# A two-layer decoder on one core: modulation chunks moved from the FFN up-projections to the attention, first tiles as unsplit fp32 products, x transposed at the end

## The chip, the core and the metric

The kernel runs on one core of one Trainium2 chip. The core has five engines that run side by side, each through its own list of instructions in order: TensorE (PE in the profile; its weight loads are PEld), VectorE (DVE), ScalarE (ACT), GpSimd (POOL) and SyncE (SP). SP issues nearly all loads. Instructions of different engines wait for one another by semaphores. The metric is the device time in microseconds (us), the median of several executions; smaller is better.

## The reference, cut to what matters

A batch of one sequence of 256 tokens with 1024 channels goes through two layers. Layer 0 mixes tokens by dilated causal attention (16 heads, three window sizes), layer 1 by gated linear attention (GLA, four heads, chunks of 64 tokens). Behind each mixer stands a gated feed-forward network (FFN) with a causal convolution over three tokens. Every one of the four sub-layers is modulated by a conditioning vector c:

```
mod = silu(c) @ w_ada[i] + b_ada[i]
sh1, sc1, g1, sh2, sc2, g2 = split(mod, 6)
h = rmsnorm(x, norm_mix[i]) * (1.0 + sc1) + sh1
y = attention(h) if i == 0 else gla(h)
x = x + g1 * y
h = rmsnorm(x, norm_ffn[i]) * (1.0 + sc2) + sh2
u = conv(h @ w_up[i]); a, b = split(u, 2)
x = x + g2 * ((silu(a) * b) @ w_down[i])
...
return rmsnorm(x, norm_final)
```

All is float32. The up-projection is 1024 to 5632, the down-projection 2816 to 1024, w_ada is 1024 to 6144 in each layer.

## The kernel before, in words

Activations lie transposed: channels on the 128 partitions, the 256 tokens along the free dimension, so x and h are eight tiles of 128x256. TensorE multiplies float32 values that are split in a high part (fp32r, a shorter float32) and a low part, the rest. `split` loads 1 MB of weights into a buffer `raw` (L159), ScalarE casts it to `whi` (L165) and VectorE subtracts to get `wlo` (L168), each in two halves of 128x1024. `mm3` (L174 to L176) then issues three matmuls: hi by hi, hi by lo, lo by hi. An unsplit fp32 matmul exists too; the kernel uses it for small things such as the sums of squares.

`raw` comes from a pool of four buffers, `whi` and `wlo` from pools of three. The matmul results go to eight banks of PSUM in three groups of tags: p (2 banks), s (3) and t (3). Where no tag is named, tags go round in a fixed cycle.

The modulation vector is made in 48 chunks, `ada_chunk` (L129 to L150), 24 a layer. A chunk loads 1 MB of w_ada into one of the same four `raw` buffers (L133). VectorE multiplies and sums each of its two halves against silu(c) (L138), and ScalarE adds the bias and writes `mod`, a column of 128 values (L146, L148). `next_ada` issues the next chunk in turn. Where the calls stand in the program decides which stage pays for them on the loads, on VectorE and on the buffers.

A norm works thus. After every tile of the residual stream is updated (`residual`, L273), `add_square` (L195) squares it on ScalarE and adds up squares. `rstd_of` (L183) sums over channels by three unsplit matmuls with a matrix of ones (`ms`, L186), then ScalarE does Ln (L188) and Exp (L190). For each of the eight tiles `normed` (L246) forms `xr` on VectorE (L250), `hhi` on ScalarE (L252) and `hlo` on VectorE (L253). While TensorE waits for the first of these, `keep_warm` (L259) issues six small matmuls without use.

The stages, in order. Layer 0's attention goes over eight pairs of heads, u = 0 to 7; in each it projects q, k (`pqk`) and v (`pv`), copies them out of PSUM (`evacuate`, L424; `by_group`, L442), and `attend` forms scores, exponentials, the normalised probabilities `pn` (L400, L401), their transposes on TensorE (L405), copies of these, `pt` (L406), and the output `po`. `project` (L515) is the output projection (`py`) with the residual. `ffn` (L539) runs 22 tiles of the up-projection: 48 matmuls into one bank `pab`, then the convolution, silu and gate product; then the down-projection (`pd`, four pairs of output tiles, four loads each). The GLA follows with the projections of v (`pv`, L649), the gates (`log_gates`), the states of four heads, four gate tiles (`gate`, L741, result `pr`), and its own `project`; then layer 1's `ffn`. At the end each tile of x is scaled by rstd (L786 to L790) and written, still transposed, by four DMAs (L791).

The order of instructions on each engine is fixed when the program is built, by a scheduler that places work by its own estimates within the dependencies; `behind(...)` is a constraint on it, which issues what stands inside after the named instructions. `chain[kt]` are the last instructions that made tile kt of h.

Of the kernel before, what the change touches and what calls it, by code (L numbers as in the profile page):

```python
# [18 lines left out]
P = 128  # L19
D = 1024  # L20
# [37 lines left out]
def trunk(ctx: ExitStack, tc: tile.TileContext, I, out):  # L58
# [136 lines left out]
    def add_square(kt):  # L195

        sq = tmp.tile([P, T], F32, tag="sq", name="sq")
        i = nc.scalar.activation(sq, x[kt], AF.Square)
        part = 0 if kt < 3 else 1 if kt < 7 else 2
        if kt in (0, 3, 7):  # L200
            sums[part] = sq
        else:
            acc = tmp.tile([P, T], F32, tag="sqacc", name="sqacc")
            (nc.gpsimd if kt < 3 else nc.vector).tensor_tensor(acc, sums[part], sq, op=ALU.add)
            sums[part] = acc
        if kt < 6:
            squared[0] = i
# [56 lines left out]

    def all_normed(l, sub):
        r = rstd_of([sums[0], sums[1], sums[2]])
        with behind(norm_ops[0]):
            keep_warm(6)
        return [normed(l, sub, r, kt) for kt in range(KT)]

    def residual(l, sub, kt, ps):
        g = mod[l, 3 * sub + 2, kt]
        i = nc.vector.scalar_tensor_tensor(x[kt], ps, g[:, 0:1], x[kt], op0=ALU.mult, op1=ALU.add)  # L273
        if kt < 6:
            squared[1] = i
# [80 lines left out]
    def attend(u, q, k, v, bias):  # L356
# [32 lines left out]
        for h in range(2):  # L389
# [6 lines left out]
            for r in (2 * h, 2 * h + 1):  # L396

                f = m[:, 12 + r : 13 + r]
                pn = att.tile([P, KEYS], F32, tag="pn", name="pn", bufs=3)
                nc.vector.tensor_scalar(grouped(pn[:, 0:T]), by_residue(prob[r][:, 0:T]), f, None, op0=ALU.mult)  # L400
                nc.vector.tensor_scalar(pn[:, T:KEYS], prob[r][:, T + r : KEYS + r], f, None, op0=ALU.mult)  # L401
                t = bank("t", "t")
                for j in range(3):
                    c = slice(P * j, P * j + P)
                    nc.tensor.transpose(t[:, c], pn[:, c], ident)  # L405
                (nc.vector.tensor_copy if r % 2 else nc.scalar.copy)(pt[:, r, :], t[:, 0:KEYS])  # L406
        po = bank("po", "t")
# [16 lines left out]
    def evacuate(q, k, g, pq, pk):  # L424
# [3 lines left out]
        if g:  # L428
            nc.scalar.mul(q[g], pq, 0.125)
            return nc.vector.tensor_copy(k[g], pk)  # L430
        qh, ql = q[0]
# [23 lines left out]
    for u in range(NPAIR):  # L455
# [53 lines left out]
        attend(u, q, k, v, bias)  # L509
        if u == 1:  # L510
            for n in range(2):
                next_ada()
    o = list(zip(o_hi, o_lo))

    def project(src, o, l, sub):  # L515

        ends = []
        for n in range(4):
            w = split(src[n], 2048)
# [10 lines left out]
            ends.append(e)  # L530
            for i in range(2):
                residual(l, sub, 2 * n + i, ps[i][:, T * i : T * i + T])
                add_square(2 * n + i)

    project(I["w_out_a"], o, 0, 0)
    at_pool.__exit__(None, None, None)


    def ffn(l):  # L539
        h = all_normed(l, 1)  # L540
        with tc.tile_pool(name=f"ffn{l}", bufs=2) as pool:
            g_hi = [pool.tile([P, T], F32R, tag=f"ghi{i}", name="ghi", bufs=1) for i in range(NFF)]
            g_lo = [pool.tile([P, T], F32R, tag=f"glo{i}", name="glo", bufs=1) for i in range(NFF)]
            for i in range(NFF):
                with behind(*(squared[:1], chain[3], chain[7])[min(i, 2)]):
                    w = split(I["w_up"][l, i], 2048)
                pab = bank("pab")
                pu = [pab[:, :T], pab[:, T:]]
                for kt in range(KT):
                    for s in range(2):  # L550
# [22 lines left out]
            exp_ln_after(silu)  # L573
            for f2 in range(0, KT, 2):
                pd = [bank("pd") for _ in range(2)]
                for half, f in ((0, 0), (0, 1), (1, 0), (1, 1)):
                    w = split(I["w_down"][l, f2 + f, half], 11 * P)
                    for j in range(11):
                        i = 11 * half + j
                        mm3(pd[f][:, :T], parts(w, P * j), (g_hi[i], g_lo[i]), i == 0, i == NFF - 1)  # L580
                for f in range(2):
                    residual(l, 1, f2 + f, pd[f][:, :T])
                    add_square(f2 + f)
                    if l == 1 and f2 + f < KT - 1:
# [4 lines left out]
    ffn(0)  # L589


# [10 lines left out]
    nc.gpsimd.memset(keep.rearrange("p (n c) -> p n c", c=CH)[:, :, 0:1], 0.0)  # L602
    h = all_normed(1, 0)

# [45 lines left out]
    for n in range(4):  # L650
        with behind(*(squared, chain[5], chain[7], glr_copy)[n]):
            w = split(I["w_v_b"][n], 2048)
            if n > 1:
                next_ada()
        for i in range(2):
            kt = 2 * n + i
# [81 lines left out]

    r_g = []

    def gate(n):  # L741
        w = split(I["w_r_b"][n], 2048)
        pr = bank("pr", "p")
        for kt in range(KT):
            for s in range(2):
                mm3(pr[:, T * s : T * s + T], parts(w, 2 * P * kt + P * s), h[kt],
                    kt == 0 and s == 0, kt == KT - 1 and s == 1)
        if n % 2 == 0:
            r_g.append(gt([P, 4, T], "r4", tag=("C", "cs")[n // 2]))
        nc.scalar.copy(r_g[-1][:, 2 * (n % 2) : 2 * (n % 2) + 2, :], pr.rearrange("p (a b) -> p a b", a=2))  # L750

# [6 lines left out]
    output(2, *s2)  # L758
    gate(0)
    next_ada()  # L760
    output(3, *s3)
    for n in range(1, 4):
        gate(n)
        if n < 2:
            next_ada()
    o = []
    for n in range(4):
        r = r_g[n // 2][:, 2 * (n % 2) : 2 * (n % 2) + 2, :]
        with behind(*norm_ops):
# [9 lines left out]
    exp_ln_after(last_hi)  # L779
    project(I["w_out_b"], o, 1, 0)  # L780
    gl_pool.__exit__(None, None, None)

    ffn(1)

    r = rstd_of([sums[0], sums[1], sums[2]])
    for kt in range(2):  # L786
        nc.gpsimd.tensor_tensor(x[kt], x[kt], r, op=ALU.mult)
    for kt in range(2, KT - 1):
        nc.vector.tensor_tensor(x[kt], x[kt], r, op=ALU.mult)
    nc.vector.scalar_tensor_tensor(x[7], x[7], col(C_NFIN + 7), r, op0=ALU.mult, op1=ALU.mult)  # L790
    for eng, a, b in ((nc.sync, 2, 4), (nc.scalar, 0, 2), (nc.sync, 4, 6), (nc.sync, 6, 8)):  # L791
        eng.dma_start(out[a:b].rearrange("k p t -> p k t"), x_all[:, a:b, :])

# [77 lines left out]
def build(arrays):  # L871
    import concourse.bacc as bacc

    nc = bacc.Bacc("TRN2", target_bir_lowering=False, num_devices=1)
# [4 lines left out]
    out = nc.dram_tensor("out_y", (KT, P, T), F32, kind="ExternalOutput").ap()  # L879
    with tile.TileContext(nc, schedule_with_timeline_sim=True) as tc:  # L880
# [12 lines left out]
```

## Time and profile before

| What | Value |
|---|---|
| median of three runs | 809.89 us (803.45 to 811.63) |
| profiled execution | 807.78 us |
| its span | 806.1 us |
| mean granted TensorE clock | 0.99 |
| PE busy | 782.4 us, 97% of the span |
| DVE busy | 645.4 us, 80% |
| ACT busy | 466.5 us, 58% |
| moved by DMA | 184.70 MB, 229 GB/s in the mean |

The stages lie in the profiled span about so: start and attention 0 to 270 us, output projection to 298, layer 0's up-projection 302 to 423 and down-projection to 487, GLA 491 to 582, its output projection to 609, layer 1's up-projection 613 to 734 and down-projection to 796, the tail to 806.

A row of the list of groups gives line, engine, operation, the tiles written and read, their shapes and the count, then the busy time in us, the mean of one in ns, and the idle time of the engine just before them with what ended it. A row of a timeline gives the start, the length, engine, line, operation and count of one burst. Matmuls are pipelined: the length of one (0.28 us for 256 columns) is longer than the distance between two starts.

### The profile page before, as it was taken

What the parts mean: (1) busy time and instruction counts of PE and PEld (TensorE: products, weight loads), DVE (VectorE), ACT (ScalarE), POOL (GpSimd) and SP (SyncE); (2) the same over time, 40 slices, a digit from 0 to 9 for tenths busy, and PEclk for the clock granted to TensorE, in tenths of its full rate; (3) what the DMA queues carried; (4) which work ended last, traced back from release to release, by engine and by line L of the source; (5) the groups of instructions that cost most, each with busy time, mean ns of one, the idle gap of its engine ahead of it and who ended that gap; (6) DMA issues with size and microseconds to landing.
All of it is one profiled execution on the core that took longest, in us unless ns stands there. A gap on an engine that the chain in (4) does not pass through costs nothing.

```text
span 806.1 us, 15899 instructions
## 1 busy us (share of the span) xinstructions
PE 782.4 (97%) x6464; PEld 752.5 (93%) x6464; DVE 645.4 (80%) x1153; ACT 466.5 (58%) x867; POOL 16.8 (2%) x42
## 2 busy tenths in 40 slices
PE   8999999999999989999999999999999999999995
PEld 6899999999999889999999998889998999999995
DVE  6998977879778769999997877776468999987552
ACT  5566555455545547777766445644556866766551
POOL 1000000000000010000000000000010000000100
PEclk9999999999999999999999999999999999999998
DMA  8998668486596736877647884873343776644521
GB/s 343 416 328 320 225 256 309 164 305 237 205 321 224 262 105 215 313 257 261 222 136 244 285 322 151 327 261 105 105 159 107 281 274 237 252 145 146 188 99 52
DMA packets 32694, 184.70 MB, mean 229 GB/s; under 512 B 5804, under 2 KB 8364, under 8 KB 15982
## 3 DMA queue, kind: packets, MB, share of 16 engines
q1 hardware_dynamic: 32350, 183.44, 63.1%
q8 instruction: 50, 0.82, 0.4%
q10 hardware_dynamic: 272, 0.26, 0.1%
q14 instruction: 22, 0.18, 0.1%
HBM read 182.59 MB, written 1.10 MB: 228 GB/s over the span
## 4 chain that ended last, share of the span: by engine, by line
PE 67%; DVE 14%; DMA 11%; ACT 4%; issue 2%; DVEq 0%; SPq 0%; ACTq 0%
PE pab L176 10%; PE pab L174 10%; PE pab L175 10%; DVE wlo L168 6%; DMA raw<-in_wqk 5%; PE pd L176 4%; PE pd L175 4%; PE pd L174 4%; PE pqk L176 3%; PE pqk L175 3%; PE pqk L174 3%; DMA raw<-in_wv 2%; DVE ada_raw L138 2%; PE py L175 2%; PE py L174 2%
## 5 line engine op out<-in xcount | busy, mean ns | idle before, releaser
L168 DVE TENSOR_TENSOR wlo<-raw,whi 128x1024 fp32r<-128x1024 f32 (+2 forms) x274 | 295.3, 1106 | 56.9 <-ACT whi L165 56.0
L165 ACT CAST whi<-raw 128x1024 fp32r<-128x1024 f32 (+2 forms) x274 | 247.9, 953 | 153.9 <-PE pab L175 50.5
L174 PE MATMUL pab<-hhi,whi 128*128 128x256 f32 x704 | 194.1, 277 | 1.5 <-ACT hhi L252 1.5
L175 PE MATMUL pab<-hlo,whi 128*128 128x256 f32 x704 | 193.9, 276 | 0.5 <-DVE hlo L253 0.5
L176 PE MATMUL pab<-hhi,wlo 128*128 128x256 f32 x704 | 194.0, 276 | 0.4 <-DVE wlo L168 0.4
L174 PEld LDWEIGHTS pab<-hhi,whi 128*128 128x128 f32 x704 | 132.0, 188 | 2.2 <-ACT hhi L252 1.9
L175 PEld LDWEIGHTS pab<-hlo,whi 128*128 128x128 f32 x704 | 132.0, 188 | 0.9 <-DVE hlo L253 0.9
L176 PEld LDWEIGHTS pab<-hhi,wlo 128*128 128x128 f32 x704 | 132.0, 188 | 0.8 <-DVE wlo L168 0.8
L174 PE MATMUL pqk<-hhi,whi 128*128 128x256 f32 x448 | 123.5, 287 | 3.0 <-ACT hhi L252 2.3
L175 PE MATMUL pqk<-hlo,whi 128*128 128x256 f32 x448 | 125.6, 284 | 0.5 <-DVE hlo L253 0.5
L176 PE MATMUL pqk<-hhi,wlo 128*128 128x256 f32 x448 | 125.0, 283 | 0.0
L138 DVE CUSTOM_DVE_ANT_0 ada_raw<-ada_raw,c_bc 128x1024 f32<-128x1024 f32 x96 | 114.1, 1224 | 5.1 <-DMA ada_raw<-in_w_ada 5.0
L176 PE MATMUL pd<-ghi,wlo 128*128 128x256 f32 x352 | 98.0, 280 | 1.5 <-DVE wlo L168 1.5
L175 PE MATMUL pd<-glo,whi 128*128 128x256 f32 x352 | 98.1, 280 | 0.0
L174 PE MATMUL pd<-ghi,whi 128*128 128x256 f32 x352 | 97.7, 279 | 0.0
L174 PEld LDWEIGHTS pqk<-hhi,whi 128*128 128x128 f32 x448 | 83.7, 191 | 4.7 <-ACT hhi L252 2.7
L175 PEld LDWEIGHTS pqk<-hlo,whi 128*128 128x128 f32 x448 | 85.4, 191 | 1.0 <-DVE hlo L253 0.7
L176 PEld LDWEIGHTS pqk<-hhi,wlo 128*128 128x128 f32 x448 | 85.1, 191 | 0.2
L176 PEld LDWEIGHTS pd<-ghi,wlo 128*128 128x128 f32 x352 | 65.8, 187 | 1.7 <-DVE wlo L168 1.7
L175 PEld LDWEIGHTS pd<-glo,whi 128*128 128x128 f32 x352 | 66.0, 188 | 0.0
L174 PEld LDWEIGHTS pd<-ghi,whi 128*128 128x128 f32 x352 | 65.9, 188 | 0.0
L558 ACT ACTIVATE r<-pab,small 128x256 f32<-128x256 f32 x88 | 48.5, 559 | 11.7 <-DVE r L561 11.3
(176 smaller groups left out, 1247.0 us busy)
## 6 DMA issues: line engine op xcount, KB each, us to landing
ada_raw<-in_w_ada SPq DMA_DIRECT2D x47, 1024.0 KB, 6.5
raw<-in_w_up SPq DMA_DIRECT2D x44, 1024.0 KB, 5.1
raw<-in_w_down SPq DMA_DIRECT2D x32, 704.0 KB, 4.2
raw<-in_wqk SPq DMA_DIRECT2D x18, 1024.0 KB, 7.0
raw<-in_wv SPq DMA_DIRECT2D x14, 768.0 KB, 4.6
raw<-in_w SPq DMA_DIRECT2D x7, 960.0 KB, 6.6
raw<-in_w_out_a SPq DMA_DIRECT2D x4, 1024.0 KB, 6.4
raw<-in_w_v_b SPq DMA_DIRECT2D x4, 1024.0 KB, 5.7
```

The lines of the kernel that those rows point to most:

```text
L138: nc.vector.tensor_tensor_reduce(w, w, c_bc, op0=ALU.mult, op1=ALU.add, scale=1.0, scalar=0.0, accum_out=dot,)
L165: copied[0] = nc.scalar.copy(hi[:, c], raw[:, c])
L168: last_lo[0] = nc.vector.tensor_tensor(lo[:, c], raw[:, c], hi[:, c].bitcast(F32), op=ALU.subtract)
L174: mm(ps, a[0], b[0], start=start, stop=False)
L175: mm(ps, a[0], b[1], start=False, stop=False)
L176: return mm(ps, a[1], b[0], start=False, stop=stop)
L558: nc.scalar.activation(r, u[:, :T], AF.Identity, scale=cw[2], bias=col(C_CB + 44 * l + f))
```

## The change

- **Modulation chunks.** Before, attention issues 20 of the 48 (two behind u = 1, three in each later pair), layer 0's up-projection 6, its down-projection 6, the GLA stage 4, layer 1's up-projection 4. The rest are made at the start. After, attention has 28 (four behind u = 1, and a fourth in each later pair), both up-projections none, layer 0's down-projection 6, the GLA stage 2, layer 1's down-projection 4.
- **Three copies to ScalarE.** In `attend` the second part of `pn` (L401, 128x128) and the odd transposes' copies (L406, 128x384), and in `evacuate` the copy of k (L430), move from VectorE.
- **Unsplit first tiles.** At three norms (both FFNs and the GLA) the first weight tile behind the norm is multiplied before rstd is known. `scale` writes x times the modulation's scale to `early_x` on ScalarE as each tile of x is done, `shift_columns` puts the shift in as column 257, `load_early` loads the weights, and `products` issues 16 unsplit fp32 matmuls of 257 columns into two banks `early`. Four of them stand ahead of the sums `ms`, twelve behind. `whole` then multiplies the result by rstd on VectorE and adds the shift's column on ScalarE. In the FFNs this is tile 0 of the up-projection, with tag p; in the GLA it is gate tile 0, with tag t. `keep_warm` isn't called any more. The `split` of tile 1 is issued behind `chain[0]`, that of tile 2 behind `chain[5]`, later ones behind `chain[7]`; `whole` in the FFN stands behind `chain[5]`.
- **The last addition.** The residual of tile 7 is issued behind the last sum of squares.
- **The end.** x is scaled by the final norm's weights and transposed on TensorE into four banks `y`, the mean square is taken with 2-column matmuls so that rstd lies on the token partitions, ScalarE and VectorE scale two banks each, and SP writes four pieces of 256 KB. The output's layout is tokens by channels, so the host's transpose goes.
- A buffer for DMA descriptors is set to 4096 bytes.

```diff
+    def products(tiles):
+        for kt in tiles:
+            for s in range(2):
+                mm(ps[s][:, 0 : T + 1], early[:, 2 * P * kt + P * s : 2 * P * kt + P * s + P], early_x[kt][:, 0 : T + 1],
+                   start=(kt == 0), stop=(kt == KT - 1))
+    products(range(2))
+    r = rstd_of([sums[0], sums[1], sums[2]], tag="t" if tag == "p" else "s")
     with behind(norm_ops[0]):
-        keep_warm(6)
+        products(range(2, KT))
+    def whole(s, out):
+        dot = tmp.tile([P, 1], F32, tag="dot", name="dot", bufs=4)
+        nc.scalar.copy(dot, ps[s][:, T : T + 1])
+        nc.vector.tensor_tensor(out, ps[s][:, 0:T], r, op=ALU.mult)
+        nc.scalar.activation(out, out, AF.Identity, bias=dot[:, 0:1])
+        return out
...
-                nc.vector.tensor_scalar(pn[:, T:KEYS], prob[r][:, T + r : KEYS + r], f, None, op0=ALU.mult)
+                nc.scalar.mul(pn[:, T:KEYS], prob[r][:, T + r : KEYS + r], f)
...
-                (nc.vector.tensor_copy if r % 2 else nc.scalar.copy)(pt[:, r, :], t[:, 0:KEYS])
+                nc.scalar.copy(pt[:, r, :], t[:, 0:KEYS])
...
-            return nc.vector.tensor_copy(k[g], pk)
+            return nc.scalar.copy(k[g], pk)
...
-        if u == 1:
-            for n in range(2):
-                next_ada()
+        for n in range((0, 4)[u] if u < 2 else 1):
+            next_ada()
...
             for i in range(NFF):
-                with behind(*(squared[:1], chain[3], chain[7])[min(i, 2)]):
-                    w = split(I["w_up"][l, i], 2048)
+                if i == 0:
+                    with behind(*chain[5]):
+                        pu = [whole(s, pool.tile([P, T], F32, tag="u", name="u")) for s in range(2)]
+                else:
+                    with behind(*((), chain[0], chain[5], chain[7])[min(i, 3)]):
+                        w = split(I["w_up"][l, i], 2048)
...
-                if i % (3, 5)[l] == 2 and i < 20:
-                    with behind(*chain[7]):
-                        next_ada()
...
                     w = split(I["w_down"][l, f2 + f, half], 11 * P)
+                    if l == 1 and (half, f) == (0, 0):
+                        next_ada()
...
+    with behind(last_pd[0]):
+        last = mean_square(range(2))
+    with behind(last):
+        last = turned(range(2))
+    with behind(last):
+        last = mean_square([2])
+    with behind(last):
+        turned(range(2, KT))
...
+            if t:
+                nc.vector.tensor_scalar(d, y_ps[t][half], r[:, 2:3], None, op0=ALU.mult)
+            else:
+                nc.scalar.mul(d, y_ps[t][half], r[:, 0:1])
+            nc.sync.dma_start(out[own, c], d)
```

More of the change, by code (lines that the diff above doesn't have):

```diff
@@ L530, in project @@
             ends.append(e)
+            if n == 3:
+                early = load_early(I["w_up"][l, 0])
             for i in range(2):
@@ L544, in ffn @@
             for i in range(NFF):
-                with behind(*(squared[:1], chain[3], chain[7])[min(i, 2)]):
-                    w = split(I["w_up"][l, i], 2048)
-                pab = bank("pab")
-                pu = [pab[:, :T], pab[:, T:]]
-                for kt in range(KT):
+                if i == 0:
[4 more added lines that the diff above has]
+                        w = split(I["w_up"][l, i], 2048)
+                    pab = bank("pab")
+                    pu = [pab[:, :T], pab[:, T:]]
+                for kt in range(KT if i else 0):
                     for s in range(2):
@@ L650, in trunk @@
     for n in range(4):
-        with behind(*(squared, chain[5], chain[7], glr_copy)[n]):
+        with behind(*(chain[0], chain[5], chain[7], glr_copy)[n]):
             w = split(I["w_v_b"][n], 2048)
@@ L654, in trunk @@
                 next_ada()
+        if n == 0:
+            with behind(*chain[5]):
+                r_g = [gt([P, 2, T], "r2")]
+                for s in range(2):
+                    whole(s, r_g[0][:, s, :])
         for i in range(2):
@@ L758, in trunk @@
     output(2, *s2)
-    gate(0)
-    next_ada()
+    gate(1)
     output(3, *s3)
-    for n in range(1, 4):
+    for n in range(2, 4):
         gate(n)
-        if n < 2:
-            next_ada()
     o = []
     for n in range(4):
-        r = r_g[n // 2][:, 2 * (n % 2) : 2 * (n % 2) + 2, :]
+        r = r_g[n]
         with behind(*norm_ops):
```

94 lines of the change are left out of this document (66 added, 28 removed).

## The prediction

> **What bounds the kernel now.** I read the windows by stage first, then the page's chain, then the timelines at the seams between stages. The columns of a window row are: stretch, its length, busy time and instructions of PE, PEld, DVE, ACT, POOL, the granted clock, the DMA share, GB/s.
>
> ```profile
> core 0: us, PE busy (x) PEld busy (x) DVE busy (x) ACT busy (x) POOL busy (x), PEclk, DMA share, GB/s
> 20.00:64.00 44.00, 42.16 (x326) 41.75 (x325) 42.61 (x69) 26.57 (x53) 0.00 (x0) 1.00 0.97 376
> 163.50:196.00 32.50, 32.50 (x280) 31.19 (x279) 25.86 (x52) 17.33 (x38) 0.20 (x2) 1.00 0.68 248
> 302.00:423.00 121.00, 120.55 (x1056) 120.00 (x1057) 117.29 (x207) 84.87 (x149) 0.00 (x0) 1.00 0.66 233
> 613.00:734.00 121.00, 120.54 (x1056) 119.99 (x1057) 114.24 (x200) 82.76 (x145) 0.00 (x0) 1.00 0.62 218
> ```
>
> PE is busy for 120.55 of 121 us in layer 0's up-projection (302 to 423), 120.54 of 121 in layer 1's, and 32.50 of 32.50 in one head pair of the attention (163.5 to 196). VectorE comes close in the up-projections (117.29 and 114.24) but TensorE doesn't wait for it there. So time is won or lost where TensorE stops: at three norms, at two places behind late operands, and in the tail.
>
> **Up-projections without modulation chunks.** Six chunks leave layer 0's and four leave layer 1's.
>
> ```profile
> L168 DVE TENSOR_TENSOR wlo<-raw,whi 128x1024 fp32r<-128x1024 f32 (+2 forms) x274 | 295.3, 1106 | 56.9 <-ACT whi L165 56.0
> L138 DVE CUSTOM_DVE_ANT_0 ada_raw<-ada_raw,c_bc 128x1024 f32<-128x1024 f32 x96 | 114.1, 1224 | 5.1 <-DMA ada_raw<-in_w_ada 5.0
> ```
>
> A chunk is two of the 1.22 us reductions of L138, so DVE loses 14.7 and 9.8 us there. TensorE has 0.45 us idle in each stage to win; I take 0 (bounds -0.5 and 0).
>
> **The two FFN norms.** Timelines of PE, DVE and ACT around layer 0's:
>
> ```profile
> 296.77 0.28 PE L176 MATMUL py<-ohi,wlo 128*128 128x256 f32 x1
> ...
> 297.83 0.28 PE L176 MATMUL py<-ohi,wlo 128*128 128x256 f32 x1
> 297.95 1.02 PE L186 MATMUL ms<-sqacc,ones_d 128*128 128x256 f32 x4
> ...
> 299.73 1.50 PE L263 MATMUL warm<-ones_d 128*128 128x128 f32 x12
> 301.97 0.38 PE L174 MATMUL pab<-hhi,whi 128*128 128x256 f32 x1 [0.74 <-ACT hhi L252]
> ```
> ```profile
> 300.44 0.42 ACT L190 ACTIVATE rstd<-ln 128x256 f32<-128x256 f32 x1
> ...
> 303.80 1.98 ACT L165 CAST whi<-raw 128x1024 fp32r<-128x1024 f32 x2
> ```
> ```profile
> 300.89 1.28 DVE L250 SCALAR_TENSOR_TENSOR xr<-x_all,mod,rstd 128x256 f32<-128x256 f32 x3 [2.26 <-ACT rstd L190]
> 302.08 0.87 DVE L253 SCALAR_TENSOR_TENSOR hlo<-xr,mod,hhi 128x256 fp32r<-128x256 f32 x2
> ...
> 304.87 1.23 DVE L168 TENSOR_TENSOR wlo<-raw,whi 128x1024 fp32r<-128x1024 f32 x1
> ```
> ```profile
> 308.76:314.20 5.44, 5.44 (x50) 5.44 (x49) 4.86 (x9) 3.91 (x6) 0.00 (x0) 1.00 0.62 206
> L186 PE MATMUL ms<-sqacc,ones_d 128*128 128x256 f32 x16 | 4.1, 379 | 0.0
> ```
>
> Before: the last py starts at 297.83, the first pab at 301.97, and the row 308.76:314.20 is tile 1 (48 matmuls, 5.44 us; the count holds neighbours' records), so tile 1 is done at 314.20. What stands there now: tile 0's 48 matmuls go (5.44 us), as do the warm ones, and 16 unsplit fp32 matmuls of 257 columns come. An unsplit 128x256 matmul is two records; four ms records last 1.02 us, the last 0.38 of it being its modelled length, so 0.21 apiece, 0.43 a matmul. With three ms: 297.95 + 16 x 0.43 + 3 x 0.43 = 306.1 to 306.2 for the last early product.
>
> In the changed program's order the early products hold both banks of tag p, and tile 1's pab takes the first of them. So its first matmul waits for the DVE multiply that reads the bank (the first `u<-early`), and this stands on DVE behind seven xr, six hlo and two wlo. rstd itself comes later: three ms stand behind four early matmuls (one inside py), and its end moves from 300.86 to about 302.0 to 302.2. From there, by the rows: xr 0.40 apiece in a run (1.28 for three, less overlap), hlo the same, wlo 1.15 to 1.23, with hlo 1 to 3 held by the hhi behind the two casts (1.98 us, now straight behind hhi 0): three xr 1.25, hlo 0.4, xr 0.4, two wlo 2.35, three hlo 1.2, three xr 1.2, two hlo 0.9, u 0.4: 8.1 us, so the first u is done at 310.1 to 310.7. TensorE idles about 4.2 us, tile 1 ends at 315.7 to 316.2 instead of 314.20: **+1.8** a norm (bounds +0.8, where only hlo 7 decides, since wlo of tile 2 and both u stand ahead of it on DVE, and +2.3).
>
> The idle time itself has a price. The rows of the one place inside the kernel where the clock fell after work had begun:
>
> ```profile
> 528.95:532.37 3.42, 1.75 (x14) 1.31 (x13) 3.42 (x8) 2.68 (x5) 0.00 (x0) 1.00 0.90 314
> 532.37:535.77 3.40, 3.40 (x17) 3.18 (x18) 3.40 (x5) 0.00 (x0) 0.00 (x0) 0.50 0.76 313
> 535.77:539.18 3.41, 3.41 (x29) 3.02 (x28) 2.83 (x7) 1.21 (x4) 0.00 (x0) 1.00 1.02 332
> ```
>
> A stretch of 3.42 us with PE busy for 1.75 was followed by 3.40 us at a clock of 0.50: half of that, 1.7 us, is lost. A gap of 4.2 us leaves any alignment of such stretches one that is idle for 2.1 us or more, so I take **+1.6** more a norm (bounds 0, if the fall needs a fully idle stretch or falls into the gap, and 2.4). Two norms: 2 x 3.4 = +6.8.
>
> [...]
>
> [...]
>
> **The GLA norm.** Here the early products use tag t and pv uses p and s, so no bank wait.
>
> ```profile
> 486.84 0.28 PE L176 MATMUL pd<-ghi,wlo 128*128 128x256 f32 x1
> ...
> 490.91 0.50 PE L174 MATMUL pv<-whi,hhi 128*128 128x512 f32 x1 [0.73 <-ACT hhi L252]
> ```
> ```profile
> 529.27 0.28 PE L176 MATMUL pqk<-hhi,wlo 128*128 128x256 f32 x1
> 530.99 0.44 PE L688 MATMUL kdt<-ident,k_d 128*128 128x128 f32 x2 [1.44 <-DVE k_d L680]
> ```
>
> pv starts 3.96 us after the slot that follows the last pd (486.95); after, 16 + 3 matmuls of 0.43, 8.2: +4.3. gate(0) goes: 48 slots of 0.118 (296.77 to 297.83 are nine), -5.65. The wait of kdt for k_d, 1.6 us between 529.27 and 530.99, shrinks to about 0.4, since the two chunks on DVE stand ahead of the gate chain there and no longer in it: -1.2, and with it the clock fall shown above most likely goes: -1.7. Sum **-4.2** (bounds -5.5 and -1.4, the latter if wait and fall stay).
>
> **Down-projections.**
>
> ```profile
> 444.56 0.28 PE L175 MATMUL pd<-glo,whi 128*128 128x256 f32 x1
> 446.33 0.39 PE L176 MATMUL pd<-ghi,wlo 128*128 128x256 f32 x1 [1.50 <-DVE wlo L168]
> ```
>
> In layer 0 one wlo is 1.5 us late behind a chunk on DVE whose load was held back by the chunk before; six chunks stay, in another order. I take -1.2 (bounds -1.7 and 0). Layer 1 gets four chunks:
>
> ```profile
> 734.00:797.00 63.00, 63.00 (x534) 62.83 (x533) 31.77 (x47) 29.44 (x49) 2.38 (x2) 1.00 0.35 118
> ```
>
> DVE has half of this stage free and 4 x 2.45 = 9.8 us fit: 0. Without that cover, one late wlo costs the 1.5 us above.
>
> **The tail.**
>
> ```profile
> 797.44 0.70 PE L186 MATMUL ms<-sq,ones_d 128*128 128x256 f32 x2 [0.16 <-ACT sq L198]
> ...
> 798.18 0.47 ACT L188 ACTIVATE ln<-ms,eps 128x256 f32<-128x256 f32 x1 [0.79 <-PE ms L186]
> 798.68 0.42 ACT L190 ACTIVATE rstd<-ln 128x256 f32<-128x256 f32 x1
> 799.13 2.82 DVE L789 TENSOR_TENSOR x_all<-x_all,rstd 128x256 f32<-128x256 f32 x5 [2.19 <-ACT rstd L190]
> ...
> 801.88 0.47 DVE L790 SCALAR_TENSOR_TENSOR x_all<-x_all,small,rstd 128x256 f32<-128x256 f32 x1
> ```
>
> From rstd (799.10) six DVE multiplies run to 802.35, then the last write goes out. After, 2-column sums, ln and exp on four columns and 16 transposes give the scale some 0.8 us sooner; four scalings of 512 columns, two each on ACT and DVE, take 2 x 0.7 or so after it (estimate from the 0.41 to 0.48 of 256 columns above), and the last of four issues, all on SP now, leaves at about 800.6. I take **-2.0** (bounds -3 and -1, where the row of four on one queue eats half).
>
> **Attention, eight more chunks, three copies to ACT.**
>
> ```profile
> L401 DVE TENSOR_SCALAR pn<-prob,m 128x128 f32<-128x128 f32 x32 | 9.1, 283 | 0.0
> L406 DVE COPY pt<-t 128x384 f32<-128x384 f32 x16 | 8.8, 549 | 1.9 <-PE t L405 1.9
> L430 DVE COPY k<-pqk 128x256 f32<-128x256 f32 x16 | 6.6, 415 | 0.1
> ```
> ```profile
> ACT whi L165 <- DMA raw<-in_wv: 30.0, 12, 3.9
> ACT whi L165 <- DMA raw<-in_wqk: 21.6, 10, 3.6
> ```
>
> A head pair gains one chunk on DVE (2.45) and loses 24.5 / 8 = 3.06: 25.9 becomes 25.3 of 32.5. ACT rises from 17.3 by about 3.5, below 21. Loads grow from 248 by 1 MB in 32.5 us, 31 GB/s, to about 280, where 376 was reached at 20 to 64. What has little room is the loop of the four raw buffers: the casts wait for wv and wqk already (30.0 and 21.6 us), and a ninth tile a head pair must pass through it. I take +1 in all (bounds -1.5, the few waits of pv and po for DVE's copies, and +10, below).
>
> The sum: 0 + 6.8 - 4.2 - 1.2 + 0 - 2.0 + 1 = +0.4. The profiled execution took 807.78 us, 0.26% under the median 809.89; on the median's ground the forecast is **810**, from 806 to 815 in its own case.
>
> **Rivals.** (1) The seams are cheap: DVE reaches u early enough that only hlo 7 decides (+0.8 a norm) and the clock holds, and the attention wins its waits: 1.6 - 5.5 - 1.8 - 3 - 1.5 = -10.2, **800**. For it speaks that DVE's set before tile 1 is mostly the same as before; against it the order on DVE, which is fixed, and the clock rows. (2) Slower: the raw buffers become the bound of the attention. The ninth tile holds one for its load and its 2.45 us on DVE; if half of that 2.45 finds no cover, a head pair is longer by 1.2, eight times: +9.8 in the attention for the +1 taken, **819**. For it speaks that the casts wait for loads in just this loop, against it PE's full 32.50 of 32.50 and the free DMA share (0.68). It decides from the point where wlo of a wqk tile ends after the last matmul of the tile before. (3) The change doesn't do what it says: the early tile only trades the norm's gap for another wait. That is already in the forecast.
>
> **How the numbers follow.** 810: 0.47; 800: 0.22, three quarters of it beyond 1% faster; 819: 0.26, nearly all of it beyond 1% slower; the rest, 0.05, on either side. One per cent (801.8 and 818.0) is about what this kernel's times can tell from no change, as the three runs lie 1% apart. Faster 0.19, same 0.51, slower 0.30. The range that leaves out no more than 2 in 10 is 798 to 821.
>
> **What would show it.** In the changed profile: TensorE idle of some 4 us between the last early product and the first pab, released by DVE `u` (no gap there: step wrong); a granted clock of 0.5 in the 3.4 us behind it; no kdt wait and no 0.5 around 532 to 536; span from rstd to the end under 6 us; head pairs of 32.5 us in the attention (33.5 or more: rival 2). The forecast is wrong if any term that I put at nothing, the up-projections above all, moves by more than 3 us.

## The result and the profile after

The changed kernel takes 815.27 us (median of seven, 811.55 to 818.18), the kernel before 809.89 us (seven, 803.45 to 811.63). The ratio taken from the runs of both is 1.0102 with a 95% interval of 1.0065 to 1.0138 (the quotient of the two medians is 1.0066): slower by about 1%, where 810 was forecast. The profiled execution of the changed kernel took 815.38 us, its span is 813.6 us, 7.5 us longer than that of before.

Where the 7.5 us come from is read from windows whose edges are the starts of the same matmuls in both profiles: the attention with its output projection (first pv to last py), the two FFN norms up to the end of tile 1, the rest of layer 0's up-projection, its down-projection, the GLA with its output projection, the rest of layer 1's up-projection, the tail (last pd to the end). A row is: stretch, its length, busy time and instructions of PE, PEld, DVE, ACT and POOL, the granted clock, the DMA share, GB/s. First the kernel before:

```profile
59.21:297.83 238.62, 235.55 (x2034) 223.10 (x2032) 193.18 (x396) 129.75 (x286) 3.63 (x14) 1.00 0.68 246
297.83:314.20 16.37, 14.96 (x117) 13.71 (x116) 13.33 (x26) 10.18 (x18) 0.00 (x0) 1.00 0.43 137
314.20:422.89 108.69, 108.69 (x961) 108.69 (x960) 105.55 (x186) 76.59 (x136) 0.00 (x0) 1.00 0.70 249
422.89:486.84 63.95, 62.45 (x531) 62.25 (x530) 47.32 (x74) 31.59 (x55) 2.01 (x2) 1.00 0.80 286
486.84:608.89 122.05, 119.04 (x861) 110.09 (x860) 83.67 (x136) 67.86 (x111) 4.24 (x8) 0.99 0.48 175
608.89:625.26 16.37, 14.98 (x117) 13.73 (x116) 13.33 (x26) 10.09 (x18) 0.00 (x0) 1.00 0.40 135
625.26:733.95 108.69, 108.69 (x961) 108.69 (x960) 102.54 (x179) 74.51 (x132) 0.00 (x0) 1.00 0.66 232
796.13:806.08 9.95, 1.85 (x9) 0.99 (x7) 3.71 (x7) 1.31 (x3) 1.83 (x2) 0.80 0.31 105
```

The same windows of the changed kernel:

```profile
59.94:306.37 246.43, 239.88 (x2036) 225.70 (x2035) 190.79 (x363) 156.70 (x377) 3.49 (x14) 0.99 0.73 272
306.37:325.19 18.82, 15.01 (x87) 13.70 (x86) 15.40 (x28) 13.44 (x32) 0.00 (x0) 0.91 0.42 164
325.19:433.88 108.69, 108.69 (x962) 108.69 (x960) 93.66 (x162) 70.96 (x121) 0.00 (x0) 1.00 0.55 186
433.88:496.06 62.18, 62.18 (x530) 62.18 (x529) 43.98 (x71) 32.33 (x61) 1.88 (x2) 1.00 0.75 272
496.06:613.93 117.87, 115.86 (x832) 106.60 (x831) 78.24 (x128) 68.28 (x124) 3.85 (x8) 1.00 0.47 172
613.93:634.41 20.48, 16.67 (x89) 15.30 (x88) 16.05 (x29) 13.60 (x25) 0.00 (x0) 0.83 0.47 166
634.41:743.10 108.69, 108.69 (x962) 108.69 (x960) 94.44 (x163) 71.05 (x124) 0.00 (x0) 1.00 0.56 190
805.28:813.58 8.30, 3.28 (x31) 3.04 (x29) 2.34 (x4) 2.27 (x5) 0.00 (x0) 0.95 0.33 126
```

Line by line, after less before, beside the term of the prediction:

| Stage | measured, us | predicted, us |
|---|---|---|
| start, up to the first pv | +0.7 | none |
| attention and its output projection | +7.8 | +1 |
| FFN norms | +2.45 and +4.11 | 2 x 3.4 |
| rest of the up-projections | 0.00 and 0.00 | 0 |
| layer 0's down-projection | -1.77 | -1.2 |
| GLA and its output projection | -4.18 | -4.2 |
| layer 1's down-projection | 0.0 | 0 |
| tail | -1.65 | -2.0 |
| sum | +7.5 | +0.4 |

The 0.7 us at the start needn't be of the change: before the first pv the same program differs by more from one execution to the next (below). So the attention is where the forecast missed. Its +7.8 is from one profile of each kernel; further profiles (below) put it between 4.6 and 9.7.

What stands at layer 0's FFN norm now, from the timelines of PE and of DVE:

```profile
306.37 0.28 PE L176 MATMUL py<-ohi,wlo 128*128 128x256 f32 x1
...
309.08 5.36 PE L291 MATMUL early<-early_x,raw 128*128 128x257 f32 x24
318.26 0.58 PE L174 MATMUL pab<-hhi,whi 128*128 128x256 f32 x1 [3.81 <-DVE u L302]
```
```profile
310.24 1.28 DVE L250 SCALAR_TENSOR_TENSOR xr<-x_all,mod,rstd 128x256 f32<-128x256 f32 x3 [3.07 <-ACT rstd L190]
...
317.78 0.75 DVE L302 TENSOR_TENSOR u<-early,rstd 128x256 f32<-128x256 f32 x2
```

The first pab waits 3.81 us, and what ends its wait is the multiply u on DVE, which starts 7.5 us behind the first xr. The clock around both norms, in windows of 3.4 us:

```profile
314.40:317.80 3.40, 0.04 (x1) 0.00 (x0) 3.40 (x10) 1.48 (x5) 0.00 (x0) 1.00 0.61 217
317.80:321.20 3.40, 2.94 (x14) 2.94 (x15) 3.40 (x7) 3.40 (x7) 0.00 (x0) 0.50 0.94 398
621.60:625.00 3.40, 0.83 (x4) 0.38 (x2) 3.40 (x8) 1.44 (x4) 0.00 (x0) 1.00 0.39 116
625.00:628.40 3.40, 2.15 (x10) 2.15 (x11) 3.40 (x8) 3.40 (x9) 0.00 (x0) 0.50 1.03 434
628.40:631.80 3.40, 3.40 (x18) 3.40 (x18) 3.40 (x5) 3.30 (x6) 0.00 (x0) 0.50 0.66 193
```

Behind each gap stands a clock of 0.50; at layer 1's it lasts for two windows, of which the first still holds 1.25 us of the gap (at layer 0's the low window holds 0.46 us of idle time, and the next, 321.20:324.60, ran at 1.00).

In the GLA and the tail:

```profile
543.00 0.44 PE L746 MATMUL kdt<-ident,k_d 128*128 128x128 f32 x2 [0.54 <-DVE k_d L738]
```
```profile
807.53 0.21 ACT L868 ACTIVATE rstd<-ln 128x4 f32<-128x4 f32 x1
807.77 1.41 ACT L877 ACTIVATE y<-y,rstd 128x512 f32<-128x512 f32 x2
807.80 1.55 DVE L875 TENSOR_SCALAR y<-y,rstd 128x512 f32<-128x512 f32 x2 [0.88 <-ACT rstd L868]
808.48 1.81 SPq L878 DMA_DIRECT2D out_y<-y  x4
```

kdt waits 0.54 us for k_d where it waited 1.44. From the end of rstd (807.74) to the last issue (its end at 810.29) are 2.55 us, where the six multiplies alone took 3.25.

In the attention, two stops of TensorE are new, and the lists of groups and of waits say two more things:

```profile
75.97 0.28 PE L175 MATMUL pqk<-hlo,whi 128*128 128x256 f32 x1
78.39 0.38 PE L176 MATMUL pqk<-hhi,wlo 128*128 128x256 f32 x1 [2.14 <-DVE wlo L168]
```
```profile
75.40:78.80 3.40, 1.26 (x14) 0.98 (x14) 3.40 (x12) 3.07 (x9) 0.20 (x2) 1.00 0.77 233
78.80:82.20 3.40, 3.40 (x18) 3.40 (x18) 3.40 (x11) 3.21 (x9) 0.00 (x0) 0.51 0.95 336
```
```profile
275.30 1.99 ACT L165 CAST whi<-raw 128x1024 fp32r<-128x1024 f32 x2 [1.59 <-DMA raw<-in_w_out_a]
...
278.53 0.39 PE L174 MATMUL py<-ohi,whi 128*128 128x256 f32 x1 [2.29 <-ACT v L488]
```
```profile
L412 PE MATMUL s<-k,q 64*64 64x64 f32 x256 | 16.5, 232 | 0.0
```
```profile
ACT whi L165 <- DMA raw<-in_wv: 13.2, 10, 1.9
ACT whi L165 <- DMA raw<-in_wqk: 5.6, 6, 1.5
ACT whi L165 <- DMA raw<-in_w_out_a: 6.0, 2, 4.4
```

At 76 us a wlo is late behind the chunks of head pair 1, which DVE does there; TensorE stops for 2.1 us and the clock is 0.51 in the 3.4 us behind it. At 276 us py waits 2.3 us for copies of v on ACT, which stand behind two casts, and the first of these had waited 1.59 us for a load of the output projection's weights. The small score matmuls (64x64) are busy for 16.5 us; the next fence, of the kernel before, has 14.8 for the same 256. And the casts of wv and wqk wait for loads less than before (13.2 for 30.0, 5.6 for 21.6), but those of the output projection's weights (w_out_a) wait more: 6.0 for the 2.0 of the second row.

```profile
L374 PE MATMUL s<-k,q 64*64 64x64 f32 x256 | 14.8, 231 | 0.0
ACT whi L165 <- DMA raw<-in_w_out_a: 2.0, 1, 2.0
```

### The profile page after: what moved, and what is told of

The parts are those of the page before. It is cut to its first block, busy times and chain, and to the rows that moved or that the text cites. A ratio compares the mean times of both kernels' runs of the same rounds, so it can differ in the third digit from the quotient of the medians.

```text
span 813.6 us, 15832 instructions
## 1 busy us (share of the span) xinstructions
PE 786.5 (97%) x6402; PEld 755.2 (93%) x6402; DVE 624.2 (77%) x1086; ACT 494.6 (61%) x986; POOL 14.3 (2%) x40
## 4 chain that ended last, share of the span: by engine, by line
PE 82%; DVE 7%; DMA 5%; ACT 4%; issue 2%; SPq 0%; ACTq 0%; DVEq 0%
PE pab L174 10%; PE pab L175 10%; PE pab L176 10%; PE pqk L174 6%; PE pqk L175 6%; PE pqk L176 6%; PE pd L175 5%; PE pd L174 5%; PE pd L176 5%; DVE wlo L168 2%; PE py L175 2%; PE py L174 2%; PE py L176 2%; PE pv L174 2%; PE pv L175 2%
## 5 line engine op out<-in xcount | busy, mean ns | idle before, releaser
L168 DVE TENSOR_TENSOR wlo<-raw,whi 128x1024 fp32r<-128x1024 f32 (+2 forms) x268 | 285.8, 1103 | 47.1 <-ACT whi L165 46.8
L165 ACT CAST whi<-raw 128x1024 fp32r<-128x1024 f32 (+2 forms) x268 | 242.1, 952 | 102.8 <-PE pab L175 36.7
L174 PE MATMUL pab<-hhi,whi 128*128 128x256 f32 x672 | 187.7, 279 | 7.6 <-DVE u L302 7.6
L175 PE MATMUL pab<-hlo,whi 128*128 128x256 f32 x672 | 187.2, 279 | 0.0
L176 PE MATMUL pab<-hhi,wlo 128*128 128x256 f32 x672 | 187.2, 279 | 0.0
L174 PEld LDWEIGHTS pab<-hhi,whi 128*128 128x128 f32 x672 | 128.1, 191 | 8.4 <-DVE u L302 8.4
L175 PEld LDWEIGHTS pab<-hlo,whi 128*128 128x128 f32 x672 | 128.1, 191 | 0.0
L176 PEld LDWEIGHTS pab<-hhi,wlo 128*128 128x128 f32 x672 | 127.9, 190 | 0.0
L606 ACT ACTIVATE r<-pab,small 128x256 f32<-128x256 f32 x84 | 45.3, 558 | 35.2 <-DVE r L609 35.2
```

The costliest lines, as they stand in the source:

```text
L165: copied[0] = nc.scalar.copy(hi[:, c], raw[:, c])
L168: last_lo[0] = nc.vector.tensor_tensor(lo[:, c], raw[:, c], hi[:, c].bitcast(F32), op=ALU.subtract)
L174: mm(ps, a[0], b[0], start=start, stop=False)
L175: mm(ps, a[0], b[1], start=False, stop=False)
L176: return mm(ps, a[1], b[0], start=False, stop=stop)
L606: nc.scalar.activation(r, u[:, :T], AF.Identity, scale=cw[2], bias=col(C_CB + 44 * l + f))
```

## The experiments

Each ratio is against the kernel before, run beside it on the same chip, since that kernel's own median differs from one sitting to the next (804 to 808 us here; 805.96 and 808.23 on one chip).

### Attention: chunks or copies (e1, e2, e3)

e1 puts all chunks back where they were, e2 the three copies, e3 both.

```diff
# e1
-        for n in range((0, 4)[u] if u < 2 else 1):
-            next_ada()
+        if u == 1:
+            for n in range(2):
+                next_ada()
...
+                if i % (3, 5)[l] == 2 and i < 20:
+                    with behind(*chain[7]):
+                        next_ada()
...
-                    if l == 1 and (half, f) == (0, 0):
-                        next_ada()
...
     gate(1)
+    next_ada()
     output(3, *s3)
     for n in range(2, 4):
         gate(n)
+        if n < 3:
+            next_ada()
# e2
-                nc.scalar.mul(pn[:, T:KEYS], prob[r][:, T + r : KEYS + r], f)
+                nc.vector.tensor_scalar(pn[:, T:KEYS], prob[r][:, T + r : KEYS + r], f, None, op0=ALU.mult)
...
-                nc.scalar.copy(pt[:, r, :], t[:, 0:KEYS])
+                (nc.vector.tensor_copy if r % 2 else nc.scalar.copy)(pt[:, r, :], t[:, 0:KEYS])
...
-            return nc.scalar.copy(k[g], pk)
+            return nc.vector.tensor_copy(k[g], pk)
```

> The changed kernel with the modulation chunks where they were before (20 in the attention, 6 and 4 in the up-projections, 4 in the GLA, none in layer 1's down-projection); the three copies stay on ScalarE. The changed kernel lost 7.8 us between the first matmul of the attention and the last of its output projection. If the eight more chunks cost that: this span shrinks by 6 to 8 us and the time is 807 to 810. If the copies (or the order of the score matmuls that comes with them) cost it: 813 to 816. The up-projections stay at 113 ns a matmul in both theories.

> The changed kernel with the three copies back on VectorE, 28 chunks in the attention. If the copies cost the 7.8 us: 807 to 810. If the chunks cost it: VectorE, now with 3 us more in a head pair, makes it worse, 815 to 819.

> Chunks and copies both as before, so only the three early tiles, the order of the norm and the tail are new. TensorE's order in the attention is then that of the kernel before. By the ledger of the traces 7.8 us go, and the chunks in the up-projections cost nothing: 806 to 809, at or under the kernel before (norms +2.5 and +4, GLA -4, down-projection -1.8, tail -1.7). If the attention's loss has another source (the early scaling on ScalarE, the weights loaded early): 811 or more.

e1: 811.70 us, ratio 1.0074 (1.0047 to 1.0102). e2: 814.55, 1.0105 (1.0070 to 1.0140). e3: 816.79, 1.0160 (1.0108 to 1.0212). So e1 lies between its two cases, e2 near the one for the chunks, and e3 beyond the 806 to 809 expected. The window of the attention and its output projection (first pv to last py) in the profiles of e1, e2 and e3, a fence each:

```profile
59.34:299.93 240.59, 239.19 (x2036) 224.41 (x2035) 173.19 (x331) 152.46 (x361) 3.48 (x14) 1.00 0.67 243
```
```profile
59.64:302.64 243.00, 239.11 (x2035) 223.72 (x2034) 209.26 (x426) 138.18 (x315) 3.44 (x14) 1.00 0.75 275
```
```profile
59.32:297.05 237.73, 235.10 (x2036) 223.04 (x2034) 190.46 (x393) 131.40 (x299) 3.50 (x14) 1.00 0.68 246
```

With neither (e3) the attention takes 237.73 us, 0.9 less than before; with the copies alone (e1) 2.9 more than e3, with the chunks alone (e2) 5.3 more, with both (the changed kernel) 8.7 more. But the same attention differs by up to 3 us from one execution to the next, as in e8, which is the changed kernel once more:

```profile
60.63:304.14 243.51, 238.27 (x2035) 224.12 (x2034) 190.72 (x363) 156.79 (x377) 3.48 (x14) 1.00 0.74 273
```

The attention of before takes 236.88 to 238.91 us in six profiles (before, e3, e7, e10, e11, e12), the changed one 243.51 to 246.53 in five (the changed kernel, e4, e5, e6, e8). So chunks and copies each cost something, e1 and e2 lying above all six, and together 4.6 to 9.7; that the chunks cost more than the copies, or that the two costs add up, one profile of each doesn't show. The stop at 276 us is in all five of the changed attention (1.0 to 2.4 us), but neither in e1 nor in e2: it takes both edits. The longer score matmuls come with either alone: 17.3 us in e1, 17.0 in e2, 14.8 in e3.

The totals don't follow the attention, and the profiles say why. e3's window is as expected, but its whole time isn't: in the GLA the order of its instructions leaves only 8 gate matmuls behind the last norm where the changed kernel has 41, and the chain from that norm to the first py lies open, as its PE timeline shows:

```profile
589.64 0.58 PE L174 MATMUL py<-ohi,whi 128*128 128x256 f32 x1 [5.72 <-ACT ohi L835]
```

The GLA window of e3 is 7.9 us longer than the changed kernel's, and the expectation of 806 to 809 was missed for that reason. The two chunks put back into the GLA don't explain it alone: e1 has them too, with 51 gate matmuls behind that norm and a wait of 0.52 us there. e3 differs from e1 only in the copies of the attention; why this moved the GLA's order stays open. e2's profile has another loss, of 4.3 us in layer 0's up-projection, to which we come back.

### The four chunks behind head pair 1 (e9)

```diff
-        for n in range((0, 4)[u] if u < 2 else 1):
+        for n in range((0, 2)[u] if u < 2 else 1):
...
+                if l == 0 and i in (4, 8):
+                    with behind(*chain[7]):
+                        next_ada()
```

> The changed kernel with two chunks behind head pair 1 instead of four; the two go to tiles 4 and 8 of layer 0's up-projection. If VectorE's four chunks in a row make the late wlo at 76 us: this stop of 2.3 us goes, the attention ends 2 to 2.5 us sooner, and the up-projection stays as long as it was. If the stop comes from something else (the copies on ScalarE, the load): it stays.

815.12 us (808.54 to 819.34), ratio 1.0128 (1.0091 to 1.0166). The profiled execution took 809.47, one of the quickest of its seven; the same window in it:

```profile
59.87:301.23 241.36, 238.76 (x2035) 223.87 (x2034) 186.28 (x355) 156.27 (x373) 3.49 (x14) 1.00 0.73 269
```

The stop at 76 us is gone, and the window is 5.1 us shorter than the changed kernel's 246.43, but only 2.2 us shorter than e8's 243.51, where the stop of 2.16 us stands and the clock of the window is 1.00 (0.99 in the changed kernel's). That is about what was expected of the stop; the rest goes with the low clock and with the stop at 276 us (0.24 us here), which differ among executions of the changed attention. The time over all runs isn't better, so the profile shows that the four chunks make the stop at 76 us, but not that moving two of them pays. The up-projection with the two chunks kept its length (108.69 us).

### The FFN norms: bank, clock, place of u (e4, e5, e6)

e4 gives the early products of the FFNs two banks of tag s, e6 also puts u behind the last hlo. e5 leaves the wait and fills it with matmuls without use.

```diff
# e4
-        h, whole = all_normed(l, 1, "p", early)
+        h, whole = all_normed(l, 1, "s", early)
...
-        r = rstd_of([sums[0], sums[1], sums[2]], tag="t" if tag == "p" else "s")
+        r = rstd_of([sums[0], sums[1], sums[2]], tag="t" if tag == "s" else "s")
# e6, with those of e4
-                    with behind(*chain[5]):
+                    with behind(*chain[7]):
                         pu = [whole(s, pool.tile([P, T], F32, tag="u", name="u")) for s in range(2)]
# e5, beside a `return e` that hands out the last matmul of `products`
...
-            products(range(2, KT))
+            last = products(range(2, KT))
+        if tag == "p":
+            with behind(last):
+                wps = bank("warm", "s")
+                for i in range(17):
+                    mm(wps[:, :P], ones_d, ones_d, start=True, stop=True)
```

> The changed kernel with the early products of the two FFN norms in two banks of tag s instead of p, so that the first matmul of tile 1 doesn't wait for VectorE's multiply u. If the bank wait is the loss, the idle 4.08 us before the first pab go to under 1 us, at both norms, the clock stays at 1.0 there, tile 1 is then bound by its last hlo (which stands behind u and two wlo): 1 to 2.5 us gained at each norm, 810 to 813. If TensorE would wait for hhi, hlo and whi just as long: the same 815.

> The changed kernel, and behind the last early product of each FFN norm 17 matmuls without use (3.8 us) into a bank of tag s, so that TensorE isn't idle while it waits for u. Nothing that the wait needs is changed. If the idle time costs a halved clock afterwards: the 3.4 us at clock 0.50 behind the two gaps go, tile 1 ends 1 to 1.7 us sooner at each norm, and 2 to 3.4 us go from the time of the changed kernel. If the clock doesn't fall because of the gap: nothing changes.

> As e4, and VectorE's two multiplies u stand behind the last hlo instead of behind hlo 5. If the place of u on VectorE is what binds tile 1 once the bank is free: another 0.5 to 0.9 us at each norm. If the two wlo of tile 2, which still stand ahead of the last hlo, bind it: the same as e4 within 0.4 us a norm.

e4: 808.89 us, ratio 1.0040 (1.0014 to 1.0067). e5: 814.44, 1.0061 (1.0020 to 1.0102). e6: 808.31, 0.9991 (0.9957 to 1.0024). The windows of the two norms, last py to the end of tile 1, in e4, e5 and e6:

```profile
304.41:319.33 14.92, 14.46 (x88) 12.81 (x86) 11.50 (x22) 10.27 (x21) 0.00 (x0) 1.00 0.37 141
612.65:627.98 15.33, 14.84 (x90) 13.15 (x88) 11.48 (x22) 10.26 (x21) 0.00 (x0) 1.00 0.38 138
```
```profile
305.56:323.21 17.65, 17.64 (x121) 16.49 (x120) 14.22 (x25) 13.00 (x32) 0.00 (x0) 1.00 0.41 147
616.27:634.15 17.88, 17.86 (x124) 16.66 (x122) 14.03 (x25) 12.71 (x24) 0.00 (x0) 1.00 0.40 142
```
```profile
307.16:321.54 14.38, 14.13 (x88) 12.69 (x86) 10.96 (x20) 9.73 (x19) 0.00 (x0) 1.00 0.38 140
611.16:625.97 14.81, 14.62 (x89) 13.13 (x88) 10.96 (x20) 9.73 (x19) 0.00 (x0) 1.00 0.36 133
```

Against 18.82 and 20.48 us in the changed kernel. e5 takes the clock alone: it stays at 1.00, and 1.2 and 2.6 us go; its total, whose interval overlaps the changed kernel's, can't show that by itself. What is left, 17.65 and 17.88, is the wait: 1.3 and 1.5 us over the kernel before. e4 takes the wait as well: 14.92 and 15.33, now 1.4 and 1.0 us under the kernel before. e6 takes another 0.5 at each, as expected of the place of u. So the early tile does what it says if its banks aren't those of the next tile, and in tag p it costs 3.9 and 5.2 us against e4. e6 also answers how much of the loss is repaired by this alone: all of it, within the interval, though its attention still takes 246.53 us; the GLA, the norms and the tail make up for that.

### A version from the parts (e7, e12), and the spread (e8, e10, e11)

e7 joins what paid: e2's copies and the chunks of before in the attention, 8 and 4 chunks in the up-projections and the changed kernel's 2 in the GLA, e6's norms, the new tail. e12 moves two of the 8 to layer 0's down-projection.

```diff
# e7, beside the edits of e2 and e6
-        for n in range((0, 4)[u] if u < 2 else 1):
-            next_ada()
+        if u == 1:
+            for n in range(2):
+                next_ada()
...
+                if (i % 2 == 0 and 2 <= i <= 16) if l == 0 else (i % 5 == 2 and i < 20):
+                    with behind(*chain[7]):
+                        next_ada()
...
-                    if l == 1 and (half, f) == (0, 0):
-                        next_ada()
# e12, against e7
-                if (i % 2 == 0 and 2 <= i <= 16) if l == 0 else (i % 5 == 2 and i < 20):
+                if i % (3, 5)[l] == 2 and i < 20:
...
-                    if l == 0 and f2 < 6:
+                    for _ in range(((2 if f and f2 < 4 else 1) if f2 < 6 else 0) if l == 0 else 0):
                         next_ada()
```

> Attention as in the kernel before (20 chunks, copies on VectorE), 8 and 4 chunks in the up-projections, 2 in the GLA, none in layer 1's down-projection; early tiles at all three norms, in tag s at the FFNs and with u behind the last hlo; the new tail. By the ledger of the traces: attention 0, norms -1.5 and -1, down-projection -1.8, GLA -4.2, tail -1.7 against the kernel before, ratio 0.985 to 0.99, if eight chunks in layer 0's up-projection still cost nothing. If chunks in the up-projection do cost: ratio 1.0.

> As e7, but 6 chunks in layer 0's up-projection as before, and the other two in its down-projection (8 there). e7's down-projection took 65.6 to 65.9 us against 62.2 in e1 and e3, which have 6 chunks in the up-projection. If the chunks' places in the up-projection make the late operands behind them: 62.3 us again and a ratio to the kernel before of 0.988 to 0.992. If eight chunks in the down-projection are themselves too many for VectorE and the loads: one or two wlo late by 1 to 2 us there, no gain on e7 (0.994).

e7: 804.03 us, ratio 0.9937 (0.9896 to 0.9978). e12: 801.44 us, ratio 0.9943 (0.9906 to 0.9980). Both are faster than both kernels, by 0.6% against the kernel before, which is less than the ledger promised: e7 lies between its two cases, and e12 in the one for no gain on e7. One reason is layer 0's down-projection, here in the profiles of e1 (6 chunks in the up-projection, 6 here), e7 (8 and 6) and e12 (6 and 8):

```profile
427.70:489.97 62.27, 62.27 (x530) 62.24 (x529) 44.18 (x71) 32.47 (x61) 1.79 (x2) 1.00 0.75 271
```
```profile
426.77:492.41 65.64, 63.99 (x531) 62.63 (x529) 50.20 (x86) 34.65 (x67) 1.66 (x2) 1.00 0.71 259
```
```profile
420.47:484.91 64.44, 63.41 (x532) 62.74 (x531) 51.90 (x88) 33.93 (x67) 2.03 (x2) 1.00 0.79 295
```

Neither place of the two chunks gets the 62.27 back; DVE is busy for 6.0 and 7.7 us more than in e1, and why the eight of e7's up-projection load the stage behind it wasn't found out (in e7, 15 of the last tiles' convolution steps on DVE still fall into this window, 8 in e1).

e8 is the changed kernel, e10 is e7 and e11 the kernel before once more, without an edit.

> The changed kernel once more, for the distance between two matmul starts in the two up-projections: 113.3 ns in both, if it is a property of the program (then 117.8 in e2, e4 and e1 comes from those edits); 117.8 in one of them, if it differs from execution to execution.

> The kernel of e7 once more, for the distance between matmul starts in layer 0's up-projection, 117.8 ns in e7's profile. If the distance belongs to the program: 117.8 again. If it differs from execution to execution: 113.3 here, and the stage 4.5 us shorter.

> The kernel before once more, for the same distance: 113.3 ns in both up-projections if it belongs to the program; 117.8 in one of them if it differs from execution to execution, which would then explain a spread of 4 to 5 us in its times. The stops at the start (12 and 20 us) should differ by up to 2 us, as they do among the profiles so far.

e8 took 814.33 us, e10 800.14, e11 805.96, a single time each. A window of 90 us amid layer 0's up-projection, where TensorE never stops, first in e7 and then in e10, which is the same program:

```profile
330.00:420.00 90.00, 90.00 (x767) 90.00 (x766) 85.41 (x150) 60.43 (x110) 0.00 (x0) 1.00 0.70 254
```
```profile
330.00:420.00 90.00, 90.00 (x796) 90.00 (x796) 88.50 (x160) 63.28 (x116) 0.00 (x0) 1.00 0.72 258
```

767 matmuls in one execution and 796 in the other, both at clock 1.00: 117.3 and 113.1 ns from start to start. Over the 961 of the stage behind tile 1 that is 4 us. e2 (766 in the same 90 us) and e4 (117.8 ns) had the slow pace in this stage, e1 in layer 1's (681 in 650:730); e5 likely had it too, since from the end of tile 1 to the last py of the next norm it took 293.06 us and the changed kernel 288.74. The first profiles of the kernel before and of the changed one have the quick pace in both stages (961 and 962 in 108.69 us). So e2's 4.3 us, and likely part of e5's total, are this pace and need not be of the edit: only e7's program was seen with both. What sets the pace stays open.

## Why the prediction was right or wrong

The range (798 to 821) held 815.27; the likeliest time, 810, and its own case, 806 to 815, just did not. In part that is luck: the excess came from the attention, where the range was wide for another reason (rival 2). In its steps:

- **Bank wait at the FFN norms.** Right. 4.2 us of idle time were worked out, 3.81 is the row; u stands where the order on DVE put it. The price apart from the clock, +1.8, measured +1.3 and +1.5 (e5). With the tag changed, 3.9 and 5.2 us go (e4).
- **Clock behind it.** Right in cause and in the mean: +1.6 taken, 1.2 and 2.6 measured (after less e5, where matmuls fill the gap and the clock stays at 1.00). The gap is 3.81 us at both norms; the window ahead of the fall had PE busy for 0.04 of 3.40 us at layer 0's (314.40:317.80) and for 0.83 of 3.40 at layer 1's (621.60:625.00). How much idle time it takes isn't settled: the stop of 2.14 us at 76 us was followed by a clock of 0.51 in the changed kernel, and in e8, with a stop of 2.16 us there, the clock of the whole attention is 1.00.
- **GLA.** Right to 0.1 us: -4.18 for -4.2. kdt waits less and no clock fall is left in that stage (its clock is 1.00, 0.99 before). e1 and e3, with four chunks in the stage, have their kdt wait of 1.6 us back; that the 1.7 us taken for the fall go with that wait isn't shown. The row has kdt 0.81 us behind the last pqk, 0.9 less than before instead of 1.2, and the early products with their sums took 8.04 us instead of 8.2: the sum is closer than its terms.
- **Tail and down-projections.** -1.65 for -2.0, -1.77 for -1.2, 0 for 0.
- **Up-projections.** 0.00 in both. Ten chunks less on DVE bought nothing.
- **Attention.** Wrong: the term was +1 and measured +7.8 (4.6 to 9.7 over all profiles). The bounds (-1.5 to +10) held it, the step didn't. It argued with sums over a head pair (DVE falls, ACT has room, loads have room), and these were true. What it left out is order: the four chunks of head pair 1 on DVE ahead of one wlo (2.1 us, and a clock of 0.51 in the 3.4 us behind it), copies of v behind two casts on ACT (2.3 us, with 1.59 us of a late load ahead of the casts), and score matmuls that the scheduler, with other lengths on DVE and ACT, puts between others in smaller groups (1.7 us more busy time for the same 256). With some 1.7 us for the low clock (an estimate, half of the 3.40 us at 0.51) these are about 8 us. e9 shows the first as the chunks'; the second takes both edits, the third comes with either; the low clock is in the changed kernel's profile and not in e8's.
- **Rival 2** had the right place, sign and nearly the size, and the wrong mechanism. In the head pairs the raw buffers aren't the bound: the casts of wv and wqk waited less for loads than before, 13.2 and 5.6 us, and from first pv to first pv five head pairs in a row (u = 2 to 6) took 30.6 to 31.8 us (29.5 to 31.3 before), not the 33.5 named as its sign. At the seam to the output projection it has a share: there the casts waited 6.0 us for loads instead of 2.0, ahead of the stop at 276 us.
- **Rival 1** is what e6 and e7 show once the banks are parted: the seams are cheap then.
- **How profile and median stand.** The spans differ by 7.5, the medians by 5.4 us. With two paces of 4 us in a stage, 3 us in the attention and 0.7 to 1.3 us at the start that differ between executions, two profiles can't fix a sum to better than that. The kernel before's own seven times fall in two groups, 803.45 to 804.55 and 809.89 to 811.63; whether that is the pace stays open, as the profile above has the quick one.

## What to carry to other kernels

Where work is pulled ahead of a wait, look first at which bank or buffer the next step takes: if it is the one that the early work holds, the wait has only moved, and here a tag was worth 3.9 and 5.2 us. A budget by stage (this engine has room for so much) doesn't price a moved instruction; what stands directly behind it on its engine, and which matmul that feeds, does. And a gap in TensorE's work was paid twice here, once as the gap and once in the clock behind it: the changed kernel's two gaps of 3.81 us were followed by 3.4 and 6.8 us at a clock of 0.50, its stop of 2.14 us by 3.4 us at 0.51, where e8, with the same stop, has 1.00 over the whole attention.

## What the runs showed of the hardware that was not expected

- In the up-projections the starts of TensorE's matmuls of 256 columns were 113 or 117 ns apart, both at a clock of 1.00, and the same program had both in two executions (330:420 holds 767 in e7 and 796 in e10). In one execution the two stages differ as well: e7 has 709 in the 80 us of 650:730, 112.8 ns.
- The low clock behind layer 1's gap lasted for two windows: 625.00:628.40 had PE busy for 2.15 of 3.40 us at 0.50, and the next 3.40 us, busy throughout, ran at 0.50 as well. Behind layer 0's, 317.80:321.20 had 2.94 of 3.40 busy at 0.50, and the next 3.40 us ran at 1.00.
- The same program had a low clock behind the stop at 76 us in one execution and not in another: 0.51 in 78.80:82.20 of the changed kernel, behind a stop of 2.14 us, and 1.00 over the whole attention of e8, with a stop of 2.16 us.
- The stretch before the first pv differs by more than a microsecond among executions of one program: it begins at 59.21 and 60.46 us in the two profiles of the kernel before, at 59.94 and 60.63 in those of the changed one.
